# Strassen's seven products for half of the contraction of a streaming encoder's input projection

## The chip, the cores and the metric

The kernel runs on one core of one Trainium2 chip. The metric is the device time of one execution in microseconds (us). Three runs of the kernel before took 1000.85, 1002.08 and 1001.82 us; the median is 1001.82 us.

Engine names in what follows: PE is TensorE's matrix multiply, PEld its weight load, DVE is VectorE, ACT is ScalarE, POOL is GpSimd, SP is SyncE, whose queue issues nearly all DMAs. L346 means line 346 of the kernel.

## The reference

One layer of a hybrid encoder over 528 tokens: 16 learned meta tokens and 512 real ones, each 2048 wide.

```python
hn = _rmsnorm(h_res, norm_in_g[l])
P = hn @ w_in[l]                                   # 2048 -> 8320 columns
Pr = Pr + (prev - Pr) * mu_shift[l]                # token shift on the first 4224 columns
r, k, v, g_r, wl, al = ...                         # 4 x 1024, 64, 64 columns of Pr
w_raw = -softplus(-(w0 + tanh(wl) @ w_lora_up)) - 0.5
decay = exp(-exp(w_raw));  a = sigmoid(a0 + al @ a_lora_up)
# recurrence over tokens, 16 heads of 64:
S = S * w_t - (S kk_t) b_t^T + v_t k_t^T;  y_t = S r_t
y_a = (groupnorm(y) + bonus) * silu(g_r)
y_b = Bg * causal_conv3(Cg * hc) * silu(g_c)       # Bg, Cg, hc, g_c: 4 x 1024 columns of P
h_res = h_res + concat([y_a, y_b]) @ w_out[l]      # 2048 -> 2048
out = _rmsnorm(h_res, norm_f_g)[:, 16:]
```

The input projection is the largest part: 65 tiles of 128 output columns (one for the low-rank inputs, 8 each of r, k, v, g, B, C, h, gc), each a contraction over 2048, that is 16 steps of 128.

## The kernel before

**Number format.** All large products are made in float32r with each operand split into a high and a low part: high is the value rounded to float32r (a copy on ACT, L158), low the difference (a subtraction on DVE or POOL, L159). A product is three matmuls: high weight by high token, high weight by low token, low weight by high token. The normed tokens are kept split in SBUF for the whole projection (`xh`, `xl`, 16 contraction steps by 528 tokens); a token's norm factor `rs` is multiplied in when a result leaves PSUM.

**A tile of the projection.** `mains` (L501) is a generator that issues one matmul after the other. Four tiles (lora, k0, r0, B0) come first together, while tokens and weights arrive. Then `main` (L358) makes one tile at a time in the order of `plan`. Tokens are the moving operand, in two ranges of 272 (or 258) and 256 columns, or one of 512 where no meta token is needed (B and gc): for k and v all 528 tokens are needed, for r, g, C and h the 512 real ones and two before them. A tile is 96 matmuls (48 for B and gc). Its results fill two of four PSUM banks (pool `pm`), so that the next tile works in the other two.

**Weights.** A tile's weights come as two DMAs of 512 KB (`prefetch`, L162) into three raw buffers, and each is split in two quarters of 512 columns into six buffers (tag `hl`): high by ACT, low by DVE for the first quarter and POOL for the second. These splits are given a priority 3000 higher than their place in the program (`WEIGHTS`); the order on DVE, ACT and POOL is otherwise the scheduler's, by priority and its own estimates. PE's order is that of the program.

**Leaving PSUM.** `use` (L419) takes a finished tile: `scaled` (L371) multiplies both ranges by `rs` on DVE; then token shift, gate or convolution follow on ACT, DVE and POOL.

**What runs between.** The heads are prepared in pairs: `prepare(i)` (L648) makes decay, keys and Gram matrices of pair i, `invert` (L873) solves the triangular systems of two pairs, `recur` (L982) runs nine chunks of the recurrence, then `split_mix` (L1126) and an output projection that already uses Strassen's seven products. All of them have short PE pieces with long chains on other engines between; PE works through the projection meanwhile. `fill(ns)` (L572) steps the generator by a fixed amount of planned time (0.43 ns a column, amounts in `FW`); `until(what, i)` (L582) steps it until that tile has been used. `later(ns, fn)` (L553) issues DMAs after so much planned time.

```python
            ns -= t
            if len(ready) > seen:
                ns += FW["evac"]
```

## Time and profile before

| | |
|---|---|
| median of three runs | 1001.82 us |
| profiled execution | 1001.71 us, span 999.9 us |
| granted TensorE clock, mean | 0.997 |
| PE busy | 988.3 us, 9723 matmuls |
| DVE busy | 685.7 us, 1247 instructions |
| ACT busy | 394.6 us, 729 instructions |
| POOL busy | 271.5 us, 292 instructions |
| DMA | 174.82 MB, mean 175 GB/s |

The page gives the busy time of each engine, the span in 40 equal slices with the busy share of each in tenths, the chain of work that ended last, the costliest groups of instructions and the DMA issues. Other views group instructions by line and shape, give the busy times of chosen stretches, or list waits and the chain in order of time. A group's row reads: line, engine, operation, tile written and tiles read, shape, count, then busy time in us and the mean of one instruction in ns, then the engine's idle time before them and what ended it. Matmuls overlap their neighbours, so the mean of one is longer than the step from one to the next.

### The profile page before, as it was taken

The numbers are of one execution on the slowest core, as the hardware profiler recorded it, in microseconds if no ns is written. First come the engines' busy times: TensorE is split into PE (matmuls) and PEld (weight loads), VectorE is DVE, ScalarE is ACT, GpSimd is POOL, SyncE is SP. The second block draws the span as 40 slices with busy tenths as digits, with TensorE's granted clock in tenths as the row PEclk, the third lists the DMA queues.
The fourth block names the chain that finished last, engine by engine and source line by source line (L and its number), as shares of the span: only waits on it lengthen the run. The fifth ranks groups of instructions, "written<-read, shape, count | busy, mean of one in ns | idle before, by whom it ended". The sixth has DMA issues, their size and how long they took to land.

```text
span 999.9 us, 23699 instructions
## 1 busy us (share of the span) xinstructions
PE 988.3 (99%) x9723; PEld 911.6 (91%) x9723; DVE 685.7 (69%) x1247; ACT 394.6 (39%) x729; POOL 271.5 (27%) x292
## 2 busy tenths in 40 slices
PE   9999999999999999999999999999999999999996
PEld 7999999999998999998999998889889898888885
DVE  6777965588765679744669644244554697997897
ACT  7553433344313434322434322222232426546463
POOL 0122423234233424232324222223332333001001
PEclk9999999999999999999999999999999999999998
DMA  9525576555575373854274846877673688797654
GB/s 329 148 85 148 132 207 171 153 144 145 141 189 165 95 193 98 203 149 119 85 197 108 197 136 192 297 215 241 204 226 99 174 264 210 187 318 175 160 127 168
DMA packets 185036, 174.82 MB, mean 175 GB/s; under 512 B 121568, under 2 KB 142816, under 8 KB 184416
## 3 DMA queue, kind: packets, MB, share of 16 engines
q1 hardware_dynamic: 182336, 164.40, 57.2%
q0 software_dynamic: 2304, 8.39, 4.8%
q8 instruction: 76, 1.25, 0.5%
q10 hardware_dynamic: 288, 0.52, 0.1%
q14 instruction: 32, 0.26, 0.1%
HBM read 136.92 MB, written 36.35 MB: 173 GB/s over the span
## 4 chain that ended last, share of the span: by engine, by line
PE 90%; DVE 5%; DMA 2%; issue 1%; SPq 0%; ACT 0%; POOL 0%; DVEq 0%; ACTq 0%; POOLq 0%
PE ps_v L346 9%; PE ps_k L346 9%; PE ps_h L346 9%; PE ps_g L346 9%; PE ps_r L346 9%; PE ps_B L346 9%; PE ps_gc L346 9%; PE ps_C L346 8%; PE M L1285 5%; PE P L1285 2%; DVE o L1256 2%; PE g L703 2%; PE Q L1285 1%; PE zs L1048 1%; PE ps_lora L346 1%
## 5 line engine op out<-in xcount | busy, mean ns | idle before, releaser
L158 ACT CAST w<-wr 128x512 fp32r<-128x512 f32 x252 | 153.0, 619 | 285.4 <-PE ps_C L346 47.3
L159 POOL TENSOR_TENSOR w<-wr,w 128x512 fp32r<-128x512 f32 x119 | 169.1, 1422 | 346.6 <-ACT w L158 289.4
L159 DVE TENSOR_TENSOR w<-wr,w 128x512 fp32r<-128x512 f32 x133 | 98.6, 747 | 114.5 <-ACT w L158 114.2
L346 PE MATMUL ps_k<-xh,w 128*128 128x272 f32 (+1 forms) x512 | 95.3, 284 | 0.0
L346 PE MATMUL ps_v<-xh,w 128*128 128x256 f32 (+1 forms) x512 | 95.3, 284 | 0.0
L346 PE MATMUL ps_r<-xh,w 128*128 128x258 f32 (+1 forms) x512 | 94.4, 281 | 0.0
L346 PE MATMUL ps_h<-xh,w 128*128 128x256 f32 (+1 forms) x512 | 94.0, 282 | 0.0
L346 PE MATMUL ps_C<-xh,w 128*128 128x256 f32 (+1 forms) x512 | 93.1, 281 | 0.0
L346 PE MATMUL ps_g<-xh,w 128*128 128x256 f32 (+1 forms) x512 | 91.5, 280 | 0.0
L346 PE MATMUL ps_B<-xh,w 128*128 128x512 f32 x256 | 83.8, 395 | 0.0
L346 PE MATMUL ps_gc<-xh,w 128*128 128x512 f32 x256 | 81.3, 392 | 0.0
L346 PEld LDWEIGHTS ps_k<-xh,w 128*128 128x128 f32 x512 | 80.0, 188 | 0.4
L346 PEld LDWEIGHTS ps_v<-xh,w 128*128 128x128 f32 x512 | 80.0, 188 | 0.3
L346 PEld LDWEIGHTS ps_h<-xh,w 128*128 128x128 f32 x512 | 79.2, 188 | 0.7
L346 PEld LDWEIGHTS ps_r<-xh,w 128*128 128x128 f32 x512 | 79.6, 188 | 0.1
L346 PEld LDWEIGHTS ps_C<-xh,w 128*128 128x128 f32 x512 | 79.2, 188 | 0.6
L346 PEld LDWEIGHTS ps_g<-xh,w 128*128 128x128 f32 x512 | 78.7, 188 | 0.2
L346 PE MATMUL ps_k<-xl,w 128*128 128x272 f32 (+1 forms) x256 | 72.6, 284 | 0.0
L346 PE MATMUL ps_v<-xl,w 128*128 128x272 f32 (+1 forms) x256 | 72.5, 283 | 0.0
L346 PE MATMUL ps_h<-xl,w 128*128 128x258 f32 (+1 forms) x256 | 71.8, 281 | 0.5 <-issue 0.5
L346 PE MATMUL ps_g<-xl,w 128*128 128x258 f32 (+1 forms) x256 | 72.0, 281 | 0.0
L346 PE MATMUL ps_r<-xl,w 128*128 128x258 f32 (+1 forms) x256 | 72.0, 281 | 0.0
(337 smaller groups left out, 2265.3 us busy)
## 6 DMA issues: line engine op xcount, KB each, us to landing
wr<-in_w_in_dram SPq DMA_DIRECT2D x126, 512.0 KB
ct<-opd SPq DMA_DIRECT2D x64, 288.0 KB
wo<-in_w_out_dram SPq DMA_DIRECT2D x24, 512.0 KB
x<-in_w_out_dram POOLq DMA_DIRECT2D x16, 512.0 KB, 6.1
opd<-ar SPq DMA_DIRECT2D x8, 576.0 KB
opd<-gt SPq DMA_DIRECT2D x16, 288.0 KB
opd<-bt SPq DMA_DIRECT2D x64, 64.0 KB
x<-in_w_out_dram SPq DMA_DIRECT2D x8, 512.0 KB
```

The lines of the kernel that those rows point to most:

```text
L158: nc.scalar.copy(hi, rq)
L159: low[q] = eng.tensor_tensor(out=lo, in0=rq, in1=hi.bitcast(F32), op=ALU.subtract).ins
L346: nc.tensor.matmul(ps[r], ww[:, w], xx[:, kt, a:b], start=(kt == 0 and n == 0), stop=(kt == KT - 1 and n == 2))
L703: nc.tensor.matmul(z[h][:, c - c0], bk[hs, c, h : h + 2, :].rearrange("p a s -> p (a s)"), ar[hs, c].rearrange("p a s -> p (a s)"), start= ...
L1048: nc.tensor.matmul(d[hs, j], w, x[hs], start=(a == 0), stop=(a == b - 1))
L1256: last = nc.vector.tensor_tensor(out=lo, in0=rq, in1=hi.bitcast(F32), op=ALU.subtract)
L1285: nc.tensor.matmul(bank[s], left(prod, jj, m, s), w, start=(jj == 0 and n == 0), stop=(jj == 7 and n == 2))
```

## The change

52 of the 65 tiles are computed in 26 pairs. For a pair (t2, t1), the first half of the contraction (steps 0 to 7) is a 2 x 2 block product: contraction steps 0 to 3 and 4 to 7, tokens in a first half S and a second half T, and the two tiles. Strassen's form (with Winograd's sums) makes it from seven products instead of eight. The second half of the contraction (steps 8 to 15) is computed as before. 13 tiles stay single: the first four, then v0, k1 and r1, and the last six. In detail:

- The tokens are laid out in two padded halves of 272 (`TB`): 256 real tokens and 16 more columns, which in the first half are zeros and in the second are the meta tokens (the two last ones first). `LX` is 544.
- Sums of token quarters are prepared: S1, S4 and S5 in SBUF of their own (`first_forms`, from a second load of the tokens), and S3 in place of the T half of steps 0 to 3 (`third_form`). After the last pair that place is loaded and split again (`restore`), since the single tiles behind it need it; the buffers of the sums are given back before the mix.
- A pair's weights are four raw DMAs of 512 KB as before (same bytes), now split into 11 parts instead of 8 quarters, four of them after an addition of two weight quarters, in place, on DVE (`sum_engine`). Lows alternate between DVE and POOL. DMAs are asked for by a part's need (`advance`, `used`).
- Each pair uses four PSUM banks, A to D, several of them more than once: after M1, P5 and Q6 ACT copies a bank to SBUF (m1, v, u2), and DVE subtracts A from v after M7.
- `scaled` first combines a bank with the saved product on DVE and then multiplies by `rs` on POOL; only one of a pair's four results is still multiplied by DVE directly from PSUM. Meta columns are separate small pieces.
- The plan's order changes with the pairs, and results of both tiles of a pair come near the pair's end.
- To make room, one `gt` buffer instead of two serves the Gram matrices (with a copy of the keys, `gk`, for even pairs, on ACT), and the low-rank weights use a buffer of the tag `tr`. The table of buffer offsets `AT_32` goes.

```diff
+PAIRED = 5
-LX = 576
+HALF, PAD = 256, 16
+TB = HALF + PAD
+LX = 2 * TB
+    first = [("lora", 0), ("k", 0), ("r", 0), ("B", 0)]
+    plan = [(("v", 0),), (("k", 1),), (("r", 1),), (("v", 1), ("g", 0)), (("g", 1), ("C", 0)), (("h", 0), ("gc", 0))]
+    for j in range(2, NPAIR, 2):
+        c = j // 2
+        plan += [(("k", j), ("v", j)), (("r", j), ("r", j + 1)), (("k", j + 1), ("v", j + 1))]
+        plan += [(("B", c - 1), ("gc", c - 1))] if c > 1 else []
+        plan += [(("g", j), ("C", c)), (("g", j + 1), ("h", c))]
+    plan += [(("B", 3), ("gc", 3))]
+    tail = [p for i in range(4, NPAIR) for p in ((("C", i), ("h", i)), (("B", i), ("gc", i)))]
+    plan += tail[:PAIRED] + [(t,) for p in tail[PAIRED:] for t in p]
...
+            raws += [m1[0], m2[0], m2[1], m1[1]]
+            add_slots(
+                p[0][0], p[0] + p[1], (n, 0, None), (n, 0, (n + 1, 0)), (n, 512, None), (n, 0, (n + 1, 512)),
+                (n + 1, 512, None), (n + 2, 0, None), (n + 1, 0, (n + 1, 512)), (n + 2, 512, None),
+                (n, 0, (n, 512)), (n + 3, 0, None), (n + 3, 512, None),
+            )
...
+        for n in range(state["slot"], min(upto, end)):
+            what, key, r, o, extra = slots[n]
+            while state["raw"] <= max(r, extra[0] if extra else 0):
+                request(state["raw"])
             with tc.high_priority(offset=WEIGHTS):
+                x = held[r][:, o : o + 512]
+                if extra:
+                    y = held[extra[0]][:, extra[1] : extra[1] + 512]
+                    sum_engine(n).tensor_tensor(out=x, in0=x, in1=y, op=ALU.add)
+                split_w(n, x, low_engine(n))
...
+    def low_engine(n):
+        return nc.gpsimd if n % 2 and 20 < n < S_IN else nc.vector
+    def sum_engine(n):
+        return nc.vector
-    pm = ph1.enter_context(tc.tile_pool(name="pm", bufs=4, space=PSUM))
+    pm = ph1.enter_context(tc.tile_pool(name="pm", bufs=1, space=PSUM))
...
+    def used():
+        state["used"] += 1
+        advance(state["used"] + 6, 2)
...
+        left = {
+            "M1": (xh, xl, 0, 0), "M2": (xh, xl, KA, 0), "P4": (xh, xl, KA, TB), "M7": (xh, xl, 0, TB),
+            "P5": sforms["S1"] + (0, 0), "Q6": sforms["S5"] + (0, 0), "M3": sforms["S4"] + (0, 0),
+        }
...
+        yield from product("M1", 0, A, HALF, True, True)
+        m1 = copy("m1", A, HALF)
+        yield from product("P5", 1, B, n_t, True, True)
+        v = copy("vv", B, n_t)
+        C = bank(perm[2], f"ps_{name}_C")
+        yield from product("M2", 2, C, HALF, True, False)
+        yield from product("Q6", 3, A, n_t, False, True)
+        u2 = copy("u2", A, HALF)
+        yield from product("M3", 4, B, HALF, False, False)
+        D = bank(perm[3], f"ps_{name}_D")
+        two = ((B, 0, HALF, False), (D, TB, n_t, True))
+        yield from straight(5, two, True, False)
+        used()
+        yield from product("M7", 6, A, n_t, False, True)
+        with ahead():
+            nc.vector.tensor_tensor(out=v[:, 0:n_t], in0=v[:, 0:n_t], in1=A[:, 0:n_t], op=ALU.subtract)
+        if len(plan[state["tile"] + 1]) == 1:
+            restore()
+            state["restored"] = True
+        yield from straight(7, two, False, True)
+        used()
+        use(*t2, (B, u2, ALU.subtract), (D, v, ALU.add))
+        yield from product("P4", 8, A, n_t, False, False)
+        state["perm"] = [perm[1], perm[3], perm[2], perm[0]]
...
+        for banks in (((C, 0, HALF, False),), ((A, TB, n_t, False),)):
+            yield from straight(9, banks, False, False)
...
+            yield from straight(10, banks, False, True)
...
+        use(*t1, (C, m1, ALU.add), (A, None, None))
...
+    def scaled(width, s, t, dst, ro, mo=0):
+        for (ps, other, op), base, n in ((s, 0, HALF), (t, TB, width)):
+            eng, x = nc.vector, ps
+            if other is not None:
+                nc.vector.tensor_tensor(out=other[:, 0:n], in0=ps[:, 0:n], in1=other[:, 0:n], op=op)
+                eng, x = nc.gpsimd, other
+            o = ro + (HALF if base else 0)
+            for a, b, d in ((0, HALF, o), (HALF, HALF + 2, mo + 14), (HALF + 2, TB, mo)):
+                if b <= n:
+                    eng.tensor_tensor(
+                        out=dst[:, d : d + b - a], in0=x[:, a:b], in1=rs[:, base + a : base + b], op=ALU.mult
+                    )
...
+    def first_forms():
...
+            a11, a21, a12, a22 = t[:, 0:2, 0:TB], t[:, 0:2, TB:LX], t[:, 2:4, 0:TB], t[:, 2:4, TB:LX]
+            nc.vector.tensor_tensor(out=a22, in0=a21, in1=a22, op=ALU.subtract)
+            nc.vector.tensor_tensor(out=a11, in0=a22, in1=a11, op=ALU.subtract)
+            nc.vector.tensor_tensor(out=a12, in0=a11, in1=a12, op=ALU.add)
+            for tag, x in (("S1", a22), ("S5", a11), ("S4", a12)):
+                hi, lo = (f[:, j : j + 2] for f in sforms[tag])
+                nc.scalar.copy(hi, x)
+                nc.vector.tensor_tensor(out=lo, in0=x, in1=hi.bitcast(F32), op=ALU.subtract)
...
+    while "restored" not in state:
+        step()
+    forms_open.close()
     pp = ctx.enter_context(tc.tile_pool(name="pp", bufs=1, side="right", reuse_waits="tile"))
```

More of the change, by code (lines that the diff above doesn't have):

```diff
@@ L133, in hymba_kernel, with halves @@
+    plan += tail[:PAIRED] + [(t,) for p in tail[PAIRED:] for t in p]
     tile_of = {"r": 0, "k": 8, "v": 16, "g": 24, "lora": 32, "B": 33, "C": 41, "h": 49, "gc": 57}
-    for what, i in plan:
+    def halves(what, i):
         m = tile_of[what] + i
-        stream += [w_in[m, :, 0:1024], w_in[m, :, 1024:2048]]
-    stream[0:8] = [stream[j] for j in (0, 2, 4, 6, 1, 3, 5, 7)]
-    N_IN = len(stream)
-    stream += [w_out[0, g] for g in range(3)]
-    quarters, chain, low = {}, {}, {}
-    state = {"next": 0, "step": 0, "banks": []}
@@ L162, in prefetch @@
[L162 to L170 removed]
+        return [w_in[m, :, 0:1024], w_in[m, :, 1024:2048]]
@@ new lines, in hymba_kernel, with add_slots @@
+    raws, slots = [], []
+    def add_slots(what, key, *entries):
+        for part, (r, o, extra) in enumerate(entries):
+            slots.append((what, key + (part,), r, o, extra))
+    for t in first:
+        raws.append(halves(*t)[0])
+    for n, t in enumerate(first):
+        slots += [(t[0], t + (q,), n, 512 * q, None) for q in range(2)]
+    for t in first:
+        n = len(raws)
+        raws.append(halves(*t)[1])
+        slots += [(t[0], t + (2 + q,), n, 512 * q, None) for q in range(2)]
@@ new lines, in hymba_kernel @@
+    N_IN, S_IN = len(raws), len(slots)
+    for g in range(3):
+        raws.append(w_out[0, g])
+        slots += [("out", ("out", g, q), N_IN + g, 512 * q, None) for q in range(2)]
+    readers = {}
+    for n, (what, key, r, o, extra) in enumerate(slots):
+        readers[r] = n
+        if extra:
+            readers[extra[0]] = max(n, readers.get(extra[0], 0))
+    quarters, chain, held = {}, {}, {}
+    state = {"raw": 4, "slot": 8, "used": 0, "banks": [], "perm": [0, 1, 2, 3], "late": False}
```

413 lines of the change are left out of this document (249 added, 164 removed).

## The prediction

> **What bounds the kernel now.** I read the page first (busy time, the 40 slices, the chain), then busy time by stages, then the chain in order of time, then the groups of instructions by engine.
>
> ```profile
> span 999.9 us, 23699 instructions
> PE 988.3 (99%) x9723; PEld 911.6 (91%) x9723; DVE 685.7 (69%) x1247; ACT 394.6 (39%) x729; POOL 271.5 (27%) x292
> PE   9999999999999999999999999999999999999996
> PEclk9999999999999999999999999999999999999998
> PE 90%; DVE 5%; DMA 2%; issue 1%; SPq 0%; ACT 0%; POOL 0%; DVEq 0%; ACTq 0%; POOLq 0%
> ```
>
> TensorE has work in every slice, at full granted clock, and is 90% of the chain. The profiled execution took 1001.71 us (span 999.9), practically the median, 1001.82, so the sum goes against 1001.7.
>
> ```profile
> 52.00:121.00 69.00, 69.00 (x587) 67.86 (x585) 56.64 (x107) 31.54 (x60) 23.34 (x29) 1.00 0.47 122
> 121.00:253.50 132.50, 132.50 (x1323) 128.89 (x1325) 93.98 (x191) 50.02 (x94) 42.60 (x50) 1.00 0.61 159
> 253.50:394.80 141.30, 141.28 (x1347) 134.80 (x1345) 97.08 (x192) 51.52 (x97) 47.55 (x52) 1.00 0.55 147
> 394.80:543.30 148.50, 148.50 (x1414) 142.50 (x1414) 95.38 (x192) 53.28 (x98) 46.89 (x51) 1.00 0.56 143
> 543.30:627.00 83.70, 83.70 (x858) 78.32 (x857) 45.26 (x97) 24.54 (x43) 20.50 (x17) 1.00 0.68 183
> 627.00:775.00 148.00, 147.11 (x2793) 131.09 (x2792) 68.99 (x119) 39.11 (x76) 44.99 (x38) 1.00 0.68 211
> 775.00:840.00 65.00, 65.00 (x380) 57.63 (x380) 50.20 (x68) 23.54 (x43) 23.97 (x17) 1.00 0.79 223
> ```
>
> These are stages (length, then PE, weight loads, DVE, ACT, POOL busy with counts, clock, DMA). 52 is the end of the first four tiles; 121, 253.5, 394.8 and 543.3 are the Gram products of the odd head pairs; at 627 the recurrence begins. DVE is busy for 388.3 us of the 575 from 52 to 627, 68%, POOL for 180.9. PE is the bound, and DVE the engine with least room.
>
> ```profile
> 120.99 1.99 PE g L703 x32
> ...
> 131.00 11.20 PE ps_C L346 x96
> ...
> 253.46 1.88 PE g L703 x32
> ...
> 380.32 11.53 PE ps_v L346 x96
> ...
> 622.04 5.93 DMA ct<-opd
> ...
> 782.71 10.88 PE ps_gc L346 x48
> ```
>
> This is the chain in order of time. A product with 512 moving columns takes 10.88/48 = 227 ns, so 256 cost 113.5. A C tile (48 with 258 columns, 48 with 256) gives 11.20/48 - 0.1135 = 120 ns for 258, a v tile likewise 127 ns for 272.
>
> **What it takes off PE.** In a pair of tiles, eight blocks of 12 products (four contraction tiles, three hi/lo terms) become seven. The one dropped is 256 wide in every kind of pair, the 258 and 272 columns staying where the meta tokens are: 12 x 113.5 ns = 1.36 us. Splitting the 512-wide B and gc products into halves costs nothing by the rate above. 26 pairs give 35.4 us; two mixed pairs carry a few wider columns than they need, 0.3 us back: 35.1. Of the 26, 21 lie before the recurrence.
>
> Is the PE time before the recurrence really shorter, when each stage is filled with a fixed amount of projection work? Adding up the planned lengths of the code (0.43 ns a column) from the Gram product of pair 1 to that of 3, of 3 to 5 and of 5 to 7, I get 112, 124 and 128 us before, 114, 109 and 112 after: before, the waits for k4 and k6 alone drew 11 and 18 us of extra tiles. So yes: the gain would come between 253 and 543, 28.6 us of it before the recurrence, provided the other engines keep up. What is left of the projection after the recurrence shrinks by only some 4 us, beside the mix where DVE is busy for 50 of 65 us: I count 3.
>
> **What it puts on DVE and POOL.** The rows for their prices:
>
> ```profile
> L159 DVE TENSOR_TENSOR w<-wr,w 128x512 fp32r<-128x512 f32 x133 | 98.6, 747 | 114.5 <-ACT w L158 114.2
> L1256 DVE TENSOR_TENSOR o<-x,o 128x512 fp32r<-128x512 f32 x58 | 37.9, 688 | 3.2 <-ACT o L1255 3.1
> L681 DVE TENSOR_TENSOR bk<-ta,e 128x576 f32<-128x576 f32 x8 | 10.1, 1266 | 0.0
> L680 DVE TENSOR_TENSOR ta<-ta,k 128x576 f32<-128x576 f32 x8 | 6.1, 759 | 5.0 <-POOL pr_v L377 2.6 <-POOL ta L674 2.4
> ```
>
> ```profile
> L159 POOL TENSOR_TENSOR w<-wr,w 128x512 fp32r<-128x512 f32 x119 | 169.1, 1422 | 346.6 <-ACT w L158 289.4 <-issue 38.6 <-DMA opd<-bt 8.6
> L444 POOL TENSOR_TENSOR u<-u,hh 128x514 f32<-128x514 f32 x8 | 10.3, 1293 | 31.9 <-DVE hh L373 31.9
> ```
>
> ```profile
> L373 DVE TENSOR_TENSOR pr_k<-ps_k,rs x16: 375/426/444, 52.7 to 516.6; 128x272 f32<-128x272 f32 x8, 128x256 f32<-128x256 f32 x8
> ```
>
> A pair has 11 weight quarters instead of 8. DVE gets four weight sums (37.9/58 = 0.65 us each, 2.6), half of three more lows (1.0), the subtraction v - A (0.4) and small pieces for the meta columns (0.2, an estimate); three of the four scalings become additions of a saved product at the same 0.42. Together 4.2 us; 21 pairs give 88 us. The token sums (S1, S4, S5 and S3) add 20 operations of 544 columns at 0.69: 14. POOL gets the other half of the lows (1.5 x 1.42) and three 256-wide scalings at half of L444's 1.29, with pieces 4.3 us a pair: 90.
>
> So from 52 to 627, DVE goes from 388 to 490 and POOL from 181 to 271, while PE wants to be through in 575 - 28.6 = 546. DVE would just fit, but the two engines hinder each other:
>
> ```profile
> 253.22 1.27 POOL L159 TENSOR_TENSOR w<-wr,w 128x512 fp32r<-128x512 f32 x1 [6.04 <-ACT w L158]
> ```
>
> ```profile
> 252.96 0.71 DVE L770 STREAM_TRANSPOSE bt<-bk 128x512 f32<-128x512 f32 x1
> 253.59 1.45 DVE L159 TENSOR_TENSOR w<-wr,w 128x512 fp32r<-128x512 f32 x1
> 254.96 0.41 DVE L373 TENSOR_TENSOR pr_g<-ps_g,rs 128x258 f32<-128x258 f32 x1
> ```
>
> POOL's low began at 253.22 and ended at 254.49; DVE's, begun at 253.59, took 1.45 us instead of 0.65 to 0.7, the rest of POOL's time more. The transpose beside it was not slowed. L681 against L680, the same operation on the same size, shows the same: 1266 against 759 ns. Taken against the shortest of its kind, DVE loses about 50 us to this between 52 and 627 (my count over the instructions). I scale it by POOL's time (271/181 = 1.50), by the time of DVE instructions with two SBUF inputs (some 210 us, to 300: 1.43) and by 575/546: 2.26 times, 63 us more. DVE then needs 553. [...]
>
> ```profile
> 375.00:400.00 25.00, 25.00 (x230) 24.84 (x229) 24.06 (x36) 11.06 (x21) 10.26 (x10) 1.00 0.39 98
> ```
>
> The fullest stretch of DVE before the recurrence is 24.06 of 25 us, 96%. At that rate 553 us take 576: against 575 before, the 28.6 us are gone, +1 in place of -28.6.
>
> **New waits in each pair.** Two chains are short. Bank C: a pair's last two blocks fill C and then A, and DVE must add m1 to C before the next pair's M2 writes C again, 2 x 12 products = 2.7 us into that pair; before, a tile's banks had a whole tile, 11 us. That addition stands in DVE's queue behind weight work of higher priority; behind it wait POOL's scaling and ACT's shift. Raw buffers: there are three, and the first raw of a pair is read until part 8, so the fourth raw (parts 9 and 10) can be asked for only after part 8 is split. Part 8 needs the buffer that M2 leaves. From M2's end: copy 0.62, low 0.75 to 1.42, a load, copy and low again; the nearest load of that size is the row `ct` above, 5.93 us. Sum 8.7 to 10.0, against 8 x 1.36 = 10.9 us to P4's end, where part 9 is due. That leaves about 1 us for DVE's queue, POOL's blocks and SP's. Lower end 0, upper end 2.5 us a pair (both delayed by one low and one sum each); I take 0.8, near the lower, since part of it falls into time that DVE is late anyway: 21 x 0.8 = 17 us.
>
> **Costs I set to nothing.** ACT gets 3 copies of 0.62 and 3 from PSUM of about 0.4 a pair, 3.1 us in 21, and is 37% busy. Six x loads for the token sums, 2.8 MB with the reload, go through SP's queue where DMA is busy for 47% (52 to 121); if they came late, P5 of the first pair would wait, a microsecond or two. The padded tokens (544 for 528) lengthen the first splits by 3%, 0.5 us at most. The single gt buffer is written again only some 30 us later.
>
> **Sum.** 1001.7 + 1 (52 to 627, DVE instead of PE) + 17 (waits in pairs) - 3 (after the recurrence) = 1017.
>
> **Rivals.**
> (a) Faster: the blocks between DVE and POOL do not grow, because POOL's work falls beside DVE's PSUM reads, which are not blocked. DVE then needs 490, 510 at 96%, under 546: PE remains the bound and 1001.7 - 28.6 - 3 = 970, with 0 to 0.8 us of waits a pair 970 to 987. It decides where the added blocking stays under 546 x 0.96 - 490 = 34 us. For it: DVE idles for 114.5 us before L159 alone, time that can be filled. Against: those idle times wait on ACT's copies, which wait on PE, and stay.
> (b) Slower by more: the short chains decide, at 2 us or more a pair; 26 x 2 = 52, in part instead of DVE's lateness: 1035 to 1060. It decides when the load takes over 7 us.
> (c) It does not save what it says on PE: the new left operands lie otherwise in SBUF. In before, 256 columns cost more in one place:
>
> ```profile
> L1494 PE MATMUL end<-home,m 128*128 128x256 f32 x48 | 5.9, 283 | 0.0
> ```
>
> 5.9/48 is about 120 ns, 6.7 more. On 84 products of 256 columns a pair that is 0.56 us, 15 over 26 pairs, a saving of 20; hidden where DVE is the bound, so 1017 to 1025. [...]
>
> **How the numbers follow.** Forecast, 1003 to 1035: 0.44. Rival (a), 966 to 999: 0.31. (b): 0.21. (c): 0.04. The range, 973 to 1055, leaves out the ends of (a) and (b). The three runs of before lie within 1.2 us, so 0.2%, 2 us, tells a change: faster 0.31, same 0.04, slower 0.65, the last from the forecast, (b) and (c) less the little that falls on the bound.
>
> **What would show it.** Right: DVE over 90% busy from 52 until the recurrence, which begins no earlier than about 625; L159's mean on DVE well above 747; PE's chain broken by waits on DVE at w, or on bank C; a pair of C and h taking 2 x 11.20 - 1.36 = 21.0 us of PE where it doesn't wait. Wrong: the recurrence begins near 600 with PE gapless. I would be wrong above all if the order on DVE leaves the blocks where nobody waits.

## The result, and the profile after

The changed kernel took 1177.38 us (median of 1174.7, 1177.38 and 1177.89) against 1001.82: a ratio of 1.175, 95% interval 1.172 to 1.178. It is slower, as forecast, but by 176 us instead of 15, and far above the range's end of 1055. The profiled execution took 1174.7 us.

The page of the changed kernel: span, busy times, PE and granted clock in 40 slices, the chain.

```profile
span 1172.9 us, 25207 instructions
PE 1022.4 (87%) x10131; PEld 961.4 (82%) x10131; DVE 832.5 (71%) x1493; ACT 476.2 (41%) x913; POOL 398.9 (34%) x438
PE   9995896896996895996896996889999899999997
PEclk9997998999999897998898999889999899999999
PE 31%; DVE 7%; DMA 4%; issue 3%; POOL 3%; ACT 2%; SPq 0%; DVEq 0%; ACTq 0%; POOLq 0%
```

PE was busy in every slice before; now it has holes from the fourth slice to the thirty-second, the granted clock drops in the same places, and PE's share of the chain falls from 90% to 31% (the shares no longer add up to the span). Busy time by stages (columns as before; 262, 431 and 611 are the Gram products of head pairs 2, 4 and 6, 129 is a time between those of pairs 0 and 1, so that the rows don't match those of before one by one):

```profile
52.00:129.00 77.00, 62.17 (x477) 59.57 (x476) 65.40 (x132) 41.84 (x78) 23.94 (x30) 0.91 0.43 125
129.00:262.00 133.00, 112.13 (x1108) 108.32 (x1107) 87.27 (x161) 47.52 (x93) 51.62 (x60) 0.94 0.39 106
262.00:431.00 169.00, 140.31 (x1330) 135.72 (x1330) 121.94 (x233) 65.73 (x130) 72.15 (x84) 0.94 0.44 118
431.00:611.00 180.00, 146.35 (x1348) 141.54 (x1347) 121.24 (x236) 65.90 (x127) 68.05 (x80) 0.90 0.41 113
52.00:780.30 728.30, 600.35 (x5588) 579.46 (x5586) 509.90 (x973) 280.45 (x543) 284.17 (x319) 0.92 0.43 118
```

The last row is the whole stretch from 52 to the recurrence, which began at 780.3 instead of 627: 153 us of the loss. In it PE was idle for 128 of 728 us (before: 0.02 of 575), at a mean clock of 0.92. By the gaps in the trace, 44.7 of the 128 lie at the products of the pairs, 36.7 at the low-rank products (tz), 25.0 at the triangular solve (t) and 19.5 at the Gram norms (n). From the recurrence to the first product of the output projection it took 228.5 us instead of 210.7, and from there to the end 164 instead of 162.

DVE was busy for 509.9 of those 728 us: 70%, hardly more than the 68% of before. POOL had 284. So the work on DVE came out near the forecast (490, or 553 with mutual hindrance), and the time did not. Where PE waited (engine, line, releaser: us in total, times, longest):

```profile
PE t L1098 <- DVE xn L1089: 25.0, 4, 7.9
PE tz L793 <- ACT luh L816: 21.7, 4, 6.3
PE n L953 <- DVE gt L921: 16.8, 6, 6.6
PE tz L794 <- DVE lul L817: 10.8, 4, 5.1
...
PE ps_g_h_B L462 <- DVE w L182: 5.5, 1, 5.5
PE ps_h_gc_C L462 <- ACT w L181: 4.7, 1, 4.7
```

The list has 31 waits of up to 5.5 us at the products of the pairs (L448, L462; the last two rows are two of them), for changing weight parts and banks: together the 44.7 us, 1.7 a pair. The largest four are none of the waits that the prediction had priced: t is the triangular solve, tz the low-rank products waiting for their split weights, n the Gram norms, whose bank now holds the meta Gram first.

Four sums help to read the runs below. I take all matmuls with 256 to 512 columns and the time from each one's start to the next start: the work at undisturbed steps (113.5, 120, 127 and 227 ns), then the excess, put to half clock where the step is 1.75 to 2.15 times the undisturbed one, to waits where it is over by more than 100 ns otherwise, and to longer steps for the rest. In us:

| | work | half clock | waits | longer steps |
|---|---|---|---|---|
| before | 893.9 | 5.8 | 7.9 | 6.2 |
| after | 859.5 | 44.0 | 102.1 | 18.9 |

The 5.8 of before are no half clock, since its trace grants half clock only in the last 7.6 us; they are short delays that fall into this class, so what counts is the difference. The saving on PE is there, 34.4 us. Against it stand 38 us more at half clock (mean granted clock 0.943 against 0.997), 94 of waits, 13 of longer steps; the remaining 62 of the 173 lie behind smaller matmuls, which this count leaves out.

### The profile page after: what moved, and what is told of

Read it like the earlier page. It is cut to its first block, busy times and chain, and to the rows that moved or that the text cites. A ratio compares the mean times of both kernels' runs of the same rounds, so it can differ in the third digit from the quotient of the medians.

```text
span 1172.9 us, 25207 instructions
## 1 busy us (share of the span) xinstructions
PE 1022.4 (87%) x10131; PEld 961.4 (82%) x10131; DVE 832.5 (71%) x1493; ACT 476.2 (41%) x913; POOL 398.9 (34%) x438
## 3 DMA queue, kind: packets, MB, share of 16 engines
q8 instruction: 79, 1.29, 0.5%
## 4 chain that ended last, share of the span: by engine, by line
PE 31%; DVE 7%; DMA 4%; issue 3%; POOL 3%; ACT 2%; SPq 0%; DVEq 0%; ACTq 0%; POOLq 0%
PE M L1491 7%; PE P L1491 4%; PE ps_gc L399 2%; PE Q L1491 2%; PE ps_B L399 2%; PE ps_C_h_A L448 1%; DMA wr<-in_w_in_dram 1%; DVE w L182 1%; PE ps_h L399 1%; PE ps_C L399 1%; PE ps_C_h_C L462 1%; PE ps_B_gc_A L448 1%; PE zy L1255 1%; POOL w L182 1%; DVE wr L200 1%
## 5 line engine op out<-in xcount | busy, mean ns | idle before, releaser
L182 POOL TENSOR_TENSOR w<-wr,w 128x512 fp32r<-128x512 f32 x159 | 227.9, 1435 | 306.7 <-ACT w L181 259.3
L181 ACT CAST w<-wr 128x512 fp32r<-128x512 f32 x330 | 197.6, 619 | 249.9 <-DMA wr<-in_w_in_dram 56.3
L182 DVE TENSOR_TENSOR w<-wr,w 128x512 fp32r<-128x512 f32 x171 | 142.1, 835 | 83.2 <-ACT w L181 80.3
L200 DVE TENSOR_TENSOR wr<-wr,wr 128x512 f32<-128x512 f32 x52 | 41.2, 792 | 28.0 <-POOL w L182 15.9
L200 DVE TENSOR_TENSOR wr<-wr 128x512 f32<-128x512 f32 x52 | 42.7, 820 | 14.7 <-POOL w L182 12.4
L1491 PE MATMUL M<-o,S 128*128 128x512 f32 x192 | 45.9, 394 | 0.0
L1491 PEld LDWEIGHTS M<-o,S 128*128 128x128 f32 x192 | 36.0, 188 | 8.6 <-DVE o L1462 0.4
L1462 DVE TENSOR_TENSOR o<-x,o 128x512 fp32r<-128x512 f32 x58 | 38.0, 687 | 2.6 <-ACT o L1461 2.3
L399 PE MATMUL ps_B<-xh,w 128*128 128x256 f32 (+1 forms) x160 | 35.1, 306 | 0.0
L448 PE MATMUL ps_k_v_A<-xh,w 128*128 128x272 f32 (+1 forms) x144 | 30.7, 293 | 1.4 <-DVE vv_k_v L489 1.4
L448 PE MATMUL ps_B_gc_A<-xh,w 128*128 128x256 f32 x120 | 24.4, 284 | 2.2 <-DVE vv_B_gc L489 2.2
L448 PEld LDWEIGHTS ps_k_v_A<-xh,w 128*128 128x128 f32 x144 | 24.2, 193 | 1.9 <-DVE vv_k_v L489 1.9
L399 PE MATMUL ps_r<-xh,w 128*128 128x258 f32 (+1 forms) x128 | 25.7, 292 | 0.0
```

Of the source, the lines that this page charges most:

```text
L181: nc.scalar.copy(hi, rq)
L182: eng.tensor_tensor(out=lo, in0=rq, in1=hi.bitcast(F32), op=ALU.subtract)
L200: sum_engine(n).tensor_tensor(out=x, in0=x, in1=y, op=ALU.add)
L399: nc.tensor.matmul(p, ww[:, w], moving(xx, kt, a, b), start=(kt == 0 and n == 0), stop=(kt == KT - 1 and n == 2))
L448: nc.tensor.matmul(ps[:, 0:c], ww[:, w], xx[:, k0 + k, o : o + c], start=(begin and k == m == 0), stop=(end and k == KA - 1 and m == 2), s ...
L1462: last = nc.vector.tensor_tensor(out=lo, in0=rq, in1=hi.bitcast(F32), op=ALU.subtract)
```

## The experiments

The kernel before, run beside them, took 1000.4 to 1001.2 us. Each time is one execution. The three runs of the changed kernel, against whose median the gains are counted, lie within 3.2 us, so smaller differences say little.

### Three side edits, alone and together

`e1_lur`: the raw low-rank weights go into buffers that are free at that time (`xo1`, `bt`) instead of one with the tag `tr`.

```diff
-        raw = tr(f"lur{i}")[:, 0 : 2 * P].rearrange("p (a b) -> p a b", a=2)
+        t = cq.tile([P, 4, CH] if i % 2 else [P, NCH - 1, 2, CH // 2, 2], F32, tag="xo1" if i % 2 else "bt", name=f"lur{i}")
+        raw = bass.AP(tensor=t.tensor, offset=t.offset, ap=[list(t.ap[0]), [P, 2], [1, P]])
```

> The changed kernel with one thing altered: the raw low-rank weights of a head pair are loaded into a buffer that is free early (xo1 or bt) instead of one of the five rotating tr buffers. The trace of after shows PE waiting 22 us for luh and 12 us for lul, in the odd pairs. Theory T (short waits of PE, one after the other, each with a cause of its own): these waits go, and the half-clock time behind them, 1177 falls by 30 to 45, to about 1140. Theory S (the prediction's: DVE and POOL have too much to do from 52 us to the recurrence, and PE waits for whatever they finish last): the waits move to the next place, less than 10 us gained, 1167 to 1180.

`e2_meta`: 2500 ns of planned projection work move between the meta Gram and the norms.

```diff
-        fill(FW["gram2"] - FW["meta"].get(i, 0))
+        fill(FW["gram2"] - FW["meta"].get(i, 0) - (0 if late else 2500))
...
             gram_meta([z[:, 384 : 384 + META] for z in zs])
+            fill(2500)
```

> The changed kernel with one thing altered: of the projection work between the Gram products and the norm sums, 2500 planned ns are moved between the Gram product of the meta tokens and the norm sums n2 that write the same banks. Same total of projection work. Theory T: the 18 us that PE waits at n for DVE's gt go, with some of the half clock, 1177 falls by 15 to 25, to about 1157. Theory S: less than 8 us gained.

`e3_scale`: the scaling of a combined result on DVE instead of POOL.

```diff
-                eng, x = nc.gpsimd, other
+                eng, x = nc.vector, other
```

> The changed kernel with one thing altered: the scaling by rs of the combined results is done by DVE instead of POOL. DVE gets about 26 x 3 instructions more (some 32 us in all), POOL 26 x 3 fewer. Theory T: the path from PSUM to the shifted k, r, v, g gets shorter, since it no longer stands behind weight lows in POOL's queue (ACT waited 74 us for pr_g and pr_k from POOL), so the time falls by 5 to 30 us. Theory S: DVE is the bound, so the time rises by 10 to 30 us, less what POOL blocks less.

`e8_three`: all three.

> The changed kernel with three single alterations together: low-rank weights in an early free buffer, 2500 planned ns of projection between the meta Gram product and n2, and the scaling by rs on DVE. Alone they gave 10, 4 and 12 us. If the waits have one cause behind them that moves from place to place, together they give about as little as the largest or the sum, 1150 to 1165. If each hid the others' gain, clearly more than the sum of 26: under 1140.

Measured: 1167.6, 1173.3, 1165.7, and together 1149.0: gains of 10, 4, 12 and 28. In e1 PE's gaps at tz go from 36.7 to 1.7 us in all, and those at the pairs' products from 44.7 to 69.3: most of what one wait gives back, the next one takes, as theory S has it. e2's 4 us are hardly more than the 3.2 by which the changed kernel's own runs differ. e3 speaks against theory S: DVE has more to do (532 us to the recurrence instead of 510), and the kernel is faster. e8 lies a microsecond under its first range: the gains add.

### DVE's load

`e4_nosum`: the changed kernel without the 104 additions of weight quarters (it leaves them out and multiplies by the unsummed quarters). `e6_load`: the kernel before with 104 operations of that size on DVE, ahead of the splits, which leave the data as they are.

```diff
-                    sum_engine(n).tensor_tensor(out=x, in0=x, in1=y, op=ALU.add)
+                    pass
```

> The changed kernel without the four additions of weight quarters per pair (104 DVE instructions, 84 us of DVE busy time in after, blocks by POOL included). The sums of weights are left out, so the products are made with unsummed weights; all else is the same. Theory S: DVE is the bound before the recurrence, so of the 70 us taken off it there most come off the time: 1177 falls to 1105 to 1125. Theory T: only the waits at weights and the head-of-line delays behind the sums get shorter, 1177 falls by 10 to 35, to 1142 to 1167.

```diff
+                if 16 <= j < 120:
+                    x = raw[:, 0:512]
+                    nc.vector.tensor_tensor(out=x, in0=x, in1=x, op=ALU.max)
```

> The kernel before with DVE load alone: 104 additional DVE instructions of 128x512 with two SBUF inputs (each raw half's first quarter replaced by the maximum of itself and itself, so values stay), with the weights' priority, ahead of the splits, from the ninth tile to the end of the projection. That is what the weight sums of 26 pairs are on DVE. Theory S: about as much as leaving out the sums took off (56 us), 1001 rises to 1030 to 1060. Theory L: the kernel before has a lead of 14 us or more and hides them, 1001 to 1010.

Measured: 1121.2 (-56) and 1033.7 (+33), both in the ranges of theory S. The additions are the largest single piece of the changed kernel that was tried. e6 from 52 to its recurrence:

```profile
52.00:644.70 592.70, 580.87 (x5519) 554.84 (x5517) 444.49 (x860) 208.87 (x388) 180.77 (x197) 1.00 0.54 143
```

DVE is at 75% in the unchanged schedule, and PE already idles for 12 us and the recurrence starts 18 us later. So the operations cost long before DVE is full. Both edits change two things, though: DVE's load, and one more operation ahead of the copy and the low of a weight part. They don't tell the two apart.

### The lead of the weights

The lead is how far ahead of PE the split weights are ready. `e5_lead`: the three token sums share one buffer (other values, same work), and the room goes to nine split buffers and four raw ones while pairs run. `e7_short`: the kernel before with four split buffers instead of six.

```diff
+        if extra_room() and state["parts"] % 9 > 5:
+            t = fp.tile([P, 2 * 512 + 48], F32R, tag="hl2", name=name, bufs=3)
...
-        advance(state["used"] + 6, 2)
+        advance(state["used"] + (9 if extra_room() else 6), 2)
...
-            sforms[tag] = (form(tag + "h"), form(tag + "l"))
+            sforms[tag] = sforms["S1"] if sforms else (form("S5h"), form("S5l"))
```

> The changed kernel with more weights ready ahead: nine split buffers instead of six and four raw buffers instead of three while pairs run. Room for them comes from leaving out part of the work's data: S1, S4 and S5 share one buffer, so that P5, M3 and Q6 read the last written sums (same instructions, other values). Theory L (lead): a pair uses a part every 1.4 us in its first half where the kernel before used a quarter every 2.8, so six buffers are a lead of 8 us, less than copy, low, sum and their queues take; with nine the waits at w and much of the half clock go, 1177 falls by 50 or more. Theory S (the order on DVE is the bound): it falls by less than 25.

```diff
-        t = wp.tile([P, 2 * 512 + 64], F32R, tag="hl", name=name, bufs=6)
+        t = wp.tile([P, 2 * 512 + 64], F32R, tag="hl", name=name, bufs=4)
```

> The kernel before with four split buffers instead of six: a lead of some 8 us at 2.8 us a quarter instead of 14, with nothing else changed. Theory L: PE waits at w as it does after the change, 1001 rises by 30 or more. Theory S: DVE has as much to do as before and fits, 1001 to 1015.

Measured: 1146.5 (-31), between the two ranges, and 1012.9 (+12), in that of theory S. Lead matters in both kernels, and settles it in neither.

### The kernel without a single pair

`e9_single`: all tiles after the first four one by one, in the order of before; the token sums aren't made.

```diff
-    plan = [(("v", 0),), (("k", 1),), (("r", 1),), (("v", 1), ("g", 0)), ...
+    plan = [(t,) for t in flat]
...
-        first_forms()
+        state["restored"] = True
```

> The changed kernel with no pair at all: its 61 tiles after the first four are computed one by one in the order of the kernel before, the sums of token quarters are not made; the padded halves, the single gt buffer, the low-rank weights in a tr buffer and the moved meta Gram stay. If the 173 us come from the pairs: about 1000 + 10 (tr buffer) + 4 (meta Gram) = 1005 to 1020. If the rest of the restructuring carries a large part: over 1050. Either way it gives the base from which a price per pair is to be counted.

Measured: 1055.1, 54 us over the kernel before with the same products, where 1005 to 1020 was expected if the loss came from the pairs. I had looked for the whole loss in them. Its waits:

```profile
PE tz L789 <- ACT luh L812: 10.0, 4, 4.6
ACT luh L812 <- DMA lur<-in_lup_dram: 9.6, 4, 3.7
...
PE tz L790 <- DVE lul L813: 7.4, 4, 2.5
```

and the stretch around one of them (length, PE, PEld, DVE, ACT, POOL, clock, DMA):

```profile
96.00:102.00 6.00, 2.02 (x17) 1.82 (x15) 4.78 (x21) 1.02 (x2) 0.88 (x4) 1.00 0.89 186
102.00:106.00 4.00, 1.51 (x7) 1.30 (x8) 3.62 (x14) 0.62 (x2) 0.23 (x1) 0.52 0.94 261
106.00:110.00 4.00, 4.00 (x23) 4.00 (x23) 2.42 (x3) 0.28 (x2) 0.00 (x0) 0.63 0.00 0
110.00:114.00 4.00, 4.00 (x35) 4.00 (x34) 1.91 (x1) 0.72 (x2) 2.93 (x2) 1.00 0.00 0
```

PE idles for 6.5 us in two pieces, then has work without a gap and yet issues 23 matmuls in 4 us instead of 35: the clock is 0.52 and 0.63 in these two rows (in the trace's own record of the clock it is 0.5 from 102.1 to 108.9). The longer of the two pieces is a wait of 4.0 us. A wait is paid a second time here. Shorter ones were followed by it too: in the changed kernel PE stood idle for 2.0 us from 503.9, and the clock was 0.5 from 506.2 to 509.6; for 2.1 us from 485.6, and it was 0.5 from 489.1 to 492.5. After 2.6 us from 200.8 it stayed at 1.00, and fell only behind another wait, of 3.8 us from 214.3. Which waits are followed by it was not shown.

Two causes were then tried by themselves. `e13_lur`: e9 with a buffer of its own for the raw low-rank weights. `e14_offsets`: the kernel before with the changed kernel's offsets in the split buffers and their size (48 spare columns instead of 64), nothing else. `e15_offsets`: e9 with the old table and buffer size. `e16_both`: e13 and e15.

```diff
-        raw = tr(f"lur{i}")[:, 0 : 2 * P].rearrange("p (a b) -> p a b", a=2)
+        raw = cq.tile([P, 2, P], F32, tag="lur", name=f"lur{i}")
```

> The kernel without pairs with the low-rank weights' raw buffer of its own again, as before the change. Theory W (the tr buffer makes the low-rank products wait, and TensorE runs at half clock after each such wait): 1055 - 20 of waits - about 12 of half clock = 1020 to 1028. If other waits take their place, as in the kernel with pairs, where the same edit brought 10: 1040 to 1050.

```diff
-    return 32 if what in ("lora", "k", "v") or part in AT_32[what][i] else 64
+    return {"out": OUT_SHIFT, "B": 16, "gc": 16, "lora": 32, "k": 32, "v": 32}.get(what, 0)
...
-        t = wp.tile([P, 2 * 512 + 64], F32R, tag="hl", name=name, bufs=6)
+        t = wp.tile([P, 2 * 512 + 48], F32R, tag="hl", name=name, bufs=6)
```

> The kernel before with the changed kernel's offsets within the split weight buffers (table removed, 0 instead of 32 or 64 for r, g, C and h) and its buffer size (48 instead of 64 spare columns), nothing else. Theory O (the place of the weights in SBUF sets the step of a matmul): the step of 256 columns goes from 113.5 to 118 ns and the time to 1001 + 13 = 1010 to 1018. If the longer steps come from the padded halves of the tokens or from another part: 1000 to 1003.

> The kernel without pairs with the offsets and the buffer size of the kernel before. Theory O: the step of 256 columns returns to 113.5 to 115 ns, 1055 - 13 = 1040 to 1045. If the offsets are not the cause, or were fitted to the old layout of the other buffers only: 1052 to 1057 with steps of 117 to 119.

> The kernel without pairs with both edits. Theories W and O together: 1001 + 8 (padded columns, moved meta Gram and what remains) = 1003 to 1013. What is left over 1001 is the price of the rest of the restructuring without pairs.

| | us | half clock | waits | longer steps | step of 256, 512 columns, ns |
|---|---|---|---|---|---|
| before | 1001 | 5.8 | 7.9 | 6.2 | 113.5, 227 |
| e9, no pairs | 1055.1 | 22.2 | 26.6 | 19.1 | 118, 231 |
| e13, own raw buffer | 1021.7 | 11.1 | 4.8 | 19.1 | 118, 231 |
| e14, before with new offsets | 1010.3 | 5.1 | 7.2 | 17.0 | 118, 231 |
| e15, e9 with old offsets | 1051.5 | 19.5 | 26.6 | 18.3 | 119, 227 |
| e16, both | 1022.9 | 12.1 | 5.6 | 18.1 | 119, 227 |

e13 and e14 came out as their first theories had it; e15 lies just under its second range, with the steps of that theory; e16 missed its 1003 to 1013, since the old offsets didn't help. The `tr` buffer is worth 33 us by itself: 22 of waits and 11 of half clock. The raw load can only be issued once a buffer of that tag is free: in e9 the load for the second head pair left SP's queue at 97.0 us, five microseconds before its product at 101.9; in e13 the same weights were split by 72 us and waited for their product at 96.4. The offsets and the buffer size, put into the kernel before, cost 9 us, and the chain of e14 shows it in a C and a gc tile (time, us, tile; before: 11.20 and 10.9):

```profile
131.25 11.35 PE ps_C L334 x96
...
153.95 11.10 PE ps_gc L334 x48
```

So where a matmul's weights lie in SBUF moves its step: 118 instead of 113.5 ns. The old offsets in the new layout (e15) bring back the 227 of the output projection but not the 113.5. That would fit a table made for the old places of the other buffers too, the tokens' among them, which no run here shows; which addresses matter stays open.

### The pairs on top of that

`e11_sixteen`: the k, v, r tiles (and v1, g0) single again, 16 pairs left. `e12_best`: the three edits and the longer lead. `e10_all`: e12 without the weight sums. `e17_bank`: e12 where P4 need not wait for DVE's reading of bank A. `e18_bare`: e10 also without v - A and without the additions of saved products, each result multiplied straight from its bank.

```diff
-        plan += [(("k", j), ("v", j)), (("r", j), ("r", j + 1)), (("k", j + 1), ("v", j + 1))]
+        plan += [((what, i),) for i in (j, j + 1) for what in ("k", "r", "v")]
```

> 16 pairs instead of 26: the k, v and r tiles (and v1, g0) are single again, in the order k, r, v; the pairs of g with C and h, of B with gc, and the five at the end stay. (The single tiles then read the sum S3 in the place of the tokens' second half of steps 0 to 3, so their values are not the reference's; the work is the same.) If each pair costs alike, from a base of about 1010 for the kernel without pairs: 1010 + 16/26 x 165 = 1110. If the cost is that of the results that come late at a pair's end and are waited for by the heads' preparation (k, v, r): 1030 to 1060. If it is the load on DVE, which falls with the pairs but not in a straight line: under 1090.

> The changed kernel with the three side edits and the longer lead, weight sums in place (the token sums still share one buffer, so the values are not the reference's). If the gains add: 1175 - 28 - 31 = 1116. If the lead heals the same waits as the side edits: 1130 to 1146. In any case over 1001: without the weight sums' 56 us there is no version with 26 pairs that beats the kernel before.

> All side edits together on the changed kernel: low-rank weights out of the tr buffer, fill between meta Gram and n2, scalings on DVE, one shared buffer for the token sums with nine split buffers and four raw ones, and no weight sums (the 104 additions are left out, and the token sums share a buffer, so those values are not the reference's). If the losses are separate and add: 1175 - 28 - 31 - 56 = 1060. If the gains overlap, since one wait takes the place of another: 1075 to 1095. If they were all that keeps TensorE from its own bound: 970 to 985. It tells how much of the loss remains with the short chains between the banks of a pair, which none of these edits touches.

```diff
-            nc.vector.tensor_tensor(out=v[:, 0:n_t], in0=v[:, 0:n_t], in1=A[:, 0:n_t], op=ALU.subtract)
+            nc.vector.tensor_tensor(out=v[:, 0:n_t], in0=v[:, 0:n_t], in1=v[:, 0:n_t], op=ALU.max)
```

> The kernel with the three side edits and the longer lead (1093), with the subtraction of bank A after M7 replaced by an operation of the same size that reads no bank (max of v with itself, so the pairs' values are wrong). P4 then need not wait for DVE before it adds to bank A. Theory B (the chains within a pair, 2.7 us of slack each): the 23 us of waits on this subtraction go, 1093 - 23 = 1070, and with less half clock down to 1062. If the delay only moves to the next place where TensorE needs DVE, since DVE is as late as before: 1083 to 1093.

```diff
-                nc.vector.tensor_tensor(out=other[:, 0:n], in0=ps[:, 0:n], in1=other[:, 0:n], op=op)
-                eng, x = nc.gpsimd, other
+                pass
```

> The same kernel without DVE's added work in the pairs: no weight sums, no v - A, no additions of the saved products (each result leaves its bank by the one multiplication, as in a single tile), so the pairs' values are wrong; the copies on ACT, the 11 splits, the bank order and the lead stay. TensorE's own bound is the 1022 of the kernel without pairs less 35, 987. Theory S (DVE's load keeps TensorE from it): 985 to 1005. If the structure of the pairs costs by itself (11 parts through nine buffers in bursts, results that come late): 1025 to 1055, most of the 1069 that remained without the weight sums.

Measured: e11 1103.0, e12 1093.3, e10 1069.2, e17 1102.2, e18 1043.0. e11 and e10 lie in none of their ranges. e12 is faster than expected: the three edits and the longer lead gain 84 us together, and 28 and 31 apart, so that each hid part of the other's gain.

e11: from the 1055 of e9, 16 pairs cost 48 us, 3.0 each; the ten more of the full kernel 74, 7.4 each. So the ten pairs whose results the heads' preparation waits for cost over twice what the others do. Whether that is why is not shown: the order of the tiles differs as well, and so does DVE's load on which the pairs are added.

e17: the waits on the subtraction (vv at L499, 17.4 us in e12 by the rows of its view, not the 23 of the expectation) vanish, and the kernel is 9 us slower, over both ranges. The replacement isn't quite neutral, since it reads SBUF alone instead of SBUF and PSUM: in the changed kernel DVE's lows, which also read SBUF alone, took 1.19 us on average where POOL was already busy and 0.69 otherwise, v - A 0.42 and 0.41. So the 9 us say little; but nothing came back: PE's gaps are 76 us in all in e12 and 81 in e17. Other waits on DVE took their place. In e12 and in e17:

```profile
PE ps_B_gc_A L458 <- DVE vv_B_gc L499: 6.8, 3, 3.8
...
PE ps_g_C_A L458 <- DVE u_B_gc L529: 3.0, 1, 3.0
...
PE ps_g_C_A L458 <- DVE u_v_g L529: 2.4, 1, 2.4
```

```profile
PE ps_g_C_A L458 <- DVE u_B_gc L529: 6.0, 1, 6.0
PE ps_g_C_A L458 <- DVE u_v_g L529: 4.9, 1, 4.9
...
PE ps_g_C_A L924 <- DVE u_B_gc L529: 3.9, 1, 3.9
```

Theory B, a cost of that one short chain, falls.

e18 brings DVE's need under the forecast's 490 us, and still misses TensorE's own bound. That bound is 1021.7 (e13) less the 34.4 of saved work, 987. From 52 to the recurrence, in e13, e18, e10 and e12:

```profile
52.00:637.00 585.00, 583.96 (x5851) 575.37 (x5850) 383.97 (x839) 215.87 (x396) 187.91 (x198) 1.00 0.54 148
```

```profile
52.00:664.00 612.00, 574.52 (x5591) 561.79 (x5589) 446.66 (x891) 278.48 (x543) 239.76 (x230) 0.96 0.52 143
```

```profile
52.00:686.00 634.00, 581.77 (x5594) 567.83 (x5592) 480.98 (x974) 278.33 (x543) 234.70 (x230) 0.95 0.50 137
```

```profile
52.00:713.40 661.40, 589.24 (x5587) 572.83 (x5586) 528.37 (x1064) 279.07 (x543) 233.82 (x230) 0.94 0.48 132
```

DVE's need of 384, 447, 481 and 528 us takes 585, 612, 634 and 661: 66, 73, 76 and 80%. From e18 to e12 each further microsecond on DVE lengthens the stretch by some 0.6 us, although DVE is idle for a fifth of it or more. (From e13 to e18 it is 0.43, while the saved products take PE's own work down.) Without pairs PE is idle for 1 us of it; with the bare pairs for 37. Of e12's distance to the bound, 106 us (1093 - 987), e18 keeps 56, a little over half; of the 144 us that DVE has more to do than in e13 it keeps 63, a little under half. So e18, in the range of the second theory, still doesn't tell a cost of the pairs' structure from one of the load that is left. That the load alone does not set the time is seen in four runs in which DVE has nearly the same to do from 52 to the recurrence:

| | DVE busy, us | stretch, us | PE idle, us |
|---|---|---|---|
| e6, no pairs, load added | 444.5 | 592.7 | 12 |
| e18, bare pairs, longer lead, side edits | 446.7 | 612.0 | 37 |
| e11, sixteen pairs, short lead | 453.2 | 646.6 | 63 |
| e4, no sums, short lead | 455.2 | 679.6 | 88 |

In e4 DVE is at 67%, less than in the kernel before, and PE idles for 88 us. The waits that remain in e18 are again for DVE, and elsewhere:

```profile
PE t L1107 <- DVE xn L1098: 13.0, 3, 5.9
PE n L921 <- DVE gt L936: 8.0, 2, 7.2
PE ps_g_C_A L458 <- DVE b L531: 4.1, 1, 4.1
PE ps_g_C_A L458 <- DVE pr_v L531: 3.8, 1, 3.8
```

With their half clock (23.1 us against 11.1 in e13) they make up most of the 56. Why DVE is late at the solve and at the Gram products with only 447 us to do, whether through the burst of results at a pair's end or through the order in its queue, was not separated further.

One way through the whole loss, each step with the one before it in place:

| | us | step |
|---|---|---|
| without pairs, own raw buffer (e13), less the saved products | 987 | |
| bare pairs (e18) | 1043 | +56 |
| with v - A and the additions of saved products (e10) | 1069 | +26 |
| with the weight sums (e12) | 1093 | +24 |
| with the shorter lead (e8) | 1149 | +56 |
| without the three side edits (the changed kernel) | 1177 | +28 |

The prices depend on the order: the sums are worth 24 here and 56 in the full kernel, the lead 56 here and 31 there, the `tr` buffer 33 without pairs and 10 with them. No version with pairs comes below the kernel before; even e18, which leaves out over half of DVE's added work, is 42 us above it. The 987 are themselves 20 us over the kernel before less the saved products (967); longer steps are 13 of these.

## Why the prediction was wrong, step by step

**PE's saving: right.** 35.1 us predicted, 34.4 in the trace. That the kernel got slower was forecast too, but not for the reason found: the sum was slower only by its 17 us of waits in the pairs, and the +1 beside them rests on the step that failed.

**Where it should come: wrong.** The stretches between the Gram products of the odd pairs, by their starts in the trace, became longer, not shorter (141.3 to 172.6 us from pair 3 to 5, 148.5 to 176.3 from 5 to 7); the gain needed PE without gaps.

**DVE's need: nearly right.** 553 us to the recurrence predicted, 509.9 measured; POOL 271 predicted, 284 measured. The hindrance is there, if smaller than taken:

```profile
L182 DVE TENSOR_TENSOR w<-wr,w 128x512 fp32r<-128x512 f32 x171 | 142.1, 835 | 83.2 <-ACT w L181 80.3
L200 DVE TENSOR_TENSOR wr<-wr,wr 128x512 f32<-128x512 f32 x52 | 41.2, 792 | 28.0 <-POOL w L182 15.9
L200 DVE TENSOR_TENSOR wr<-wr 128x512 f32<-128x512 f32 x52 | 42.7, 820 | 14.7 <-POOL w L182 12.4
```

The lows take 835 ns for 747, the sums some 0.8 us for the 0.65 I took. The reading of L681 was half of it: of its eight instructions four took 1.60 to 1.85 us, where a low of POOL's had begun about 0.3 us earlier, and four 0.75 to 0.76, where the two began within 0.13 us of each other, and POOL's low took 1.88 to 2.38 instead of 1.29 to 1.57. So in these eight either delayed the other, POOL's low DVE where it was well under way.

**"At that rate 553 us take 576": this is the step that failed.** I took the length of the stretch from the sum of DVE's work, at the share (96%) of its fullest 25 us, so that PE would lose only what DVE has too much to do. DVE had less to do than that, 509.9 us, and the stretch took 728, with PE idle for 128: PE waits for single results that come late, not for DVE's sum. DVE itself stands still for 218 us of the stretch, 52.6 of them until ACT's copy of a weight part is there and 21.5 until POOL's low is, ahead of a sum. No other share would have served as the rate: in the stretches compared above DVE reached 66 to 80%, and with nearly the same need, 445 to 455 us, they took 593 to 680. What moved the time in the experiments was the lead (e5, e7), the shared buffer (e13) and operations on DVE in the weights' way (e4, e6). That all of these act through single results that come late fits PE's list of waits, and is argued from it. Why DVE is late at the solve and the Gram products stays open.

**Short waits, 0.8 us a pair: too small.** The waits of the pairs' own products come to 1.7 us a pair, inside the bounds of 0 and 2.5 but at twice the value taken; and 96 us more of waits lie elsewhere, 83 of them before the recurrence. Two chains were missing in my list: bank A (P4 after v - A) and the first bank after the m1 copy. In place of one price per pair there is a lateness, mostly of DVE, that surfaces at whichever place is next (e1, e17).

**Costs set to nothing: wrong in two places, perhaps three.** The low-rank weights in a `tr` buffer (33 us without pairs), which I described and did not price; the removed table of offsets (9 us), which I took for bookkeeping; and perhaps the meta Gram in the norms' banks (e2: 4, barely clear of the runs' spread; in e9, without pairs, PE waits there for 1 us). For the single gt buffer and the token loads no wait of PE shows.

**Half clock: not in the sum at all.** The trace of before has none until its last 7.6 us, and I priced each wait once. It added 38 us.

**Rivals.** (b), slower through the short chains, named the right sign and place, and its 2 us a pair are near the 1.7 measured; alone that explains a quarter of the loss. (c), longer steps by a new layout, came true (12.7 us; I had 15), and not hidden. The places of the split weights alone bring it about (e14, 10.8 us); whether the new places of the tokens have a part in it is open (e15). (5.9/48 in (c) is 123 ns; from start to start those matmuls take 120.)

**The signs I named.** DVE over 90% busy: no, 70%. Recurrence no earlier than 625: yes, 780. L159's mean above 747: yes, 835. PE's chain broken by waits at w or a bank: yes, among others. A pair of C and h in 21.0 us: not to be read, since the three such pairs come beside the recurrence, with its short products in between.

## What to carry to other kernels

The busy time that an engine reaches in its fullest window is no rate for a stretch, and neither is its share over a whole one: here 445 to 455 us of DVE's work went with 12 to 88 us of idle time on PE. Look instead at each result that the bound engine needs, and at how long before that the work on it can begin. A change that takes room from elsewhere is priced also there: who now shares the buffer, when its load can be issued, which offsets were fitted. And the matmul engine's waits cost about one and a half times in these runs, for the clock that follows them (22 us of waits and 11 of half clock in e9 over e13; 94 and 38 in the changed kernel).

## What the runs showed of the hardware

- The place of the split weights in SBUF moves the matmul's step from 113.5 to 118 ns (256 columns) and from 227 to 231 (512), with nothing else changed than their offsets and the size of their buffers (e14); the step of 272 columns fell from 127 to 125. This run doesn't show how the offset acts, but it does act.
- With PE idle for 6.5 of the 10 us from 96, the mean clock was 0.52 from 102 to 106 and 0.63 from 106 to 110 (e9). In the changed kernel a wait of 2.0 us (from 503.9) and one of 2.1 (from 485.6) were followed by 3.4 us at 0.5 each, one of 2.6 (from 200.8) by none; half clock added 38 us.
- DVE and POOL, each in an operation with two SBUF inputs, delayed each other: where POOL had begun about 0.3 us earlier, 0.76 us of DVE became 1.60 to 1.85; where the two began within 0.13 us, POOL took 1.88 to 2.38 instead of 1.29 to 1.57 (L681 and L159 of the kernel before). DVE's scalings of 256 columns from PSUM took 0.42 us there on average, whether POOL was already busy or not (L373), as rival (a) had it.
